# A hybrid decoder step on one core: copies shared by two engines lean to ScalarE, a guard folded into a multiplication, squares cast by ScalarE, and the first steps of the triangular inverses in one instruction each

## The chip, the core and the metric

The kernel runs on one core of a Trainium2 chip. A core has TensorE (PE in the profile, with its weight loads as PEld), VectorE (DVE), ScalarE (ACT), GpSimd (POOL) and SyncE (SP, which only issues DMAs here). Each engine works through its own list of instructions in the order in which the program wrote them, and engines wait for one another by semaphores. The metric is the device time of one execution in microseconds; the profile comes from one further execution.

## The reference, cut to what matters

One decoder layer for a prompt of 1024 tokens and 8 single-token samples: one wide projection of x (1024 features to about 9,360 columns), then two recurrent branches (gated linear attention, "GLA", with 4 heads, and RWKV-7 with 16 heads of 64), a gated merge, an output projection and a layer norm. The part that the change touches is RWKV-7's keys and its recurrence:

```python
kk = hr(kb * rwkv_k_k)
kk = kk / jnp.maximum(jnp.sqrt(jnp.sum(jnp.square(kk), axis=-1, keepdims=True)), L2_EPS)
kb = kb * (1.0 + (a - 1.0) * rwkv_k_a)
...
def step(S, inp):
    rt, wt, kt, vt, kkt, at = inp
    sa = jnp.einsum('bhvk,bhk->bhv', S, -kkt)
    S = S * wt[:, :, None, :] + sa[..., None] * (kkt * at)[:, :, None, :] + vt[..., None] * kt[:, :, None, :]
    y = jnp.einsum('bhvk,bhk->bhv', S, rt)
    return S, y
```

`kk` is each head's key, scaled per channel and normalized over the head's 64 channels, with a guard (`L2_EPS` is 1e-12) against a zero norm.

## The kernel before, in words

All matrix products of the projections are done in three passes with a high and a low part of both operands (`xs` for x, `wpart` for weights; the high part is a rounded copy that ScalarE casts, the low part the difference that VectorE or GpSimd forms). The prompt is worked in two halves of 512 tokens ("contexts" 0 and 1; context 0 carries the 8 samples too, and its rows are 256 and 264 columns wide, while those of context 1 are 512 wide). For each half `make_plan` lists the rows of the projection; between them stand the RWKV pairs (two heads each, 8 pairs per half) and the 4 GLA heads. After the two halves follow the up-projections of both branches (`up_row`) and the output projection with the norm (`out`).

One RWKV pair goes through `pair`: `front` forms decays, normalized keys and the products of the chunked form (chunks of 64 tokens, 8 per half), and solves for 32x32 triangular inverses on VectorE; `back` and `turn` join the blocks and transpose; `chain` walks over the 8 chunks one after the other, and each chunk makes three trips from TensorE to a copying engine and back: `pr` (PSUM tile `pch`) is copied to `rh`, then `pu` is copied to `u` (the tile `wide`; one copy for each head), then `pS` is scaled and added into the next `u` on VectorE. `norm` follows.

In `front`, `head_sums` sums the squared keys over a head with a matrix product by a block matrix of ones: `split` makes a rounded high part and a low part of the squares, each as an own pass of TensorE. The sums come back in PSUM; before, VectorE then takes the maximum with 1e-24, and ScalarE takes logarithm and exponential for the inverse root. The inverse's loop over `j` in `front` makes two VectorE instructions in every step, a product into `Xt` and an addition into `X`. Of its 31 steps the first four have one block row only (`ni == 1`).

The order of the instructions is made by a planner in the file (`Order.run`): streams of operations compete, and the one with the smallest key (start by the planner's own prices, less a priority) is written next on its engine. Operations made through `self.C` can go to ScalarE or VectorE, those through `self.E` to VectorE or GpSimd; `Order.start` takes the way whose end comes first by the planner's prices, after adding `BIAS` to VectorE's end if ScalarE is the first choice:

```python
end = t + cost
if len(op.ways) > 1:
    end += BIAS if eng == "V" and "A" in op.ways[0][0] else ASIDE if eng == "G" and "G" in op.port else 0.0
```

So `BIAS` is the number of planned microseconds by which VectorE must be sooner to get a shared copy. Every choice moves the planned times after it, so the whole order is written anew when one number changes. ScalarE's Sigmoid and Tanh need another table than Exp and Ln; the planner writes the table loads (line 401). Most instructions are written at one line (L217), so groups are told apart by their tiles.

Of the kernel before, what the change touches and what calls it, by code (L numbers as in the profile page):

```python
# [14 lines left out]
AF = mybir.ActivationFunctionType  # L15
ALU = mybir.AluOpType
# [16 lines left out]
C = 64  # L33
# [40 lines left out]

SPARE = 0.4
LANDED = 0.5
BIAS = 0.1
ASIDE = 0.5

PRIO = {"evacuate": 0.7, "pair": 0.4, "turn": 0.5, "chain": 0.5, "norm": 0.1, "x": 0.7, "lora": 0.2, "rank": -0.3,  # L80
# [16 lines left out]
KK_SCALE = 65536.0  # L97
# [325 lines left out]
class Kern(Order):  # L423
# [41 lines left out]
        o, w = CST[name]  # L465
        return self.cons[:, o:o + w]

    def split(self, x, tag="part"):

        hi, lo = (t[:x.shape[0], :x.free_size()] for t in (yield from self.get(tag, 2)))  # L470
        yield self.C.copy(hi, x)
        yield (self.V if x.space == PSUM else self.E).tensor_sub(lo, x, hi.bitcast(F32))
        return hi, lo

# [5 lines left out]
    def blocks32(self, x):  # L480
        return x.rearrange("p (j f) -> p j f", f=32)

    def head_sums(self, x):

        hi, lo = yield from self.split(x)
        ps = yield from self.bank("big", [P, HT])
        yield from self.sums(ps, self.headsr, hi, lo)
        self.free(hi, lo)
        return ps
# [6 lines left out]
    def setup(self):  # L496
        nc, a = self.nc, self.a
        E = mybir.EngineType
        self.es.enter_context(self.tc.manual_schedule(engines={E.PE, E.Activation, E.DVE, E.Pool, E.SP}))
        cp = self.pool("const")  # L500
        wp = self.pool("w", side="left")
        self.dr = self.pool("dr", space=DRAM)
        pp = self.pool("psum", space=PSUM)
        xp = self.pool("x", side="right")
        self.r1 = r1 = self.pool("work", side="left")
        for tag, bufs in BANKS.items():
            self.buffers(tag, bufs, lambda tag=tag, bufs=bufs: pp.tile([P, 512], F32, name=tag, bufs=bufs))
        for tag, (shape, bufs) in SBUF.items():
            dt = F32R if tag in PARTS else F32
            self.buffers(tag, bufs, lambda tag=tag, shape=shape, bufs=bufs, dt=dt:  # L510
                         r1.tile(shape, dt, name=tag, bufs=bufs))
        for tag, (shape, bufs) in WBUF.items():
            dt = F32 if tag == "wraw" else F32R
            self.buffers(tag, bufs, lambda tag=tag, shape=shape, bufs=bufs, dt=dt:
                         wp.tile(shape, dt, name=tag, bufs=bufs))
        self.buffers("xs", XS, lambda: xp.tile([P, HALF], F32R, name="xs", bufs=XS))
        nc.scalar.preload_act_table_set(EXP)
        self.cons = cp.tile([P, CST_W], F32, name="cons")
        self.pv = cp.tile([P, PV_W], F32, name="pv")
        self.ident = self.cst("ident")  # L520
        self.omu = cp.tile([P, NRC], F32, name="omu")
        self.oka = cp.tile([P, 8], F32, name="oka")
        self.nkk = cp.tile([P, 8], F32, name="nkk")
        self.bias = {}
        for n, v in [("glaeps", GLA_EPS), ("gneps", GN_EPS), ("lneps", LN_EPS), ("one", 1.0),
                     ("kkl", 0.5 * math.log(KK_SCALE))]:
            t = cp.tile([P, 1], F32, name="b_" + n)
            nc.vector.memset(t, v)
            self.bias[n] = t
        dbg = getattr(self, "dbg", {})  # L530
        self.o_gla = dbg.get("o_gla", None) or self.dr.tile([D, T], F32, name="o_gla")
        self.o_rwkv = dbg.get("o_rwkv", None) or self.dr.tile([D, T], F32, name="o_rwkv")
        self.sg = [[[self.dr.tile([P, PASS[i][1]], F32, name=f"sg{i}{n}{k}") for k in range(NK)] for n in range(2)]
                   for i in range(2)]
        self.mg = [[self.dr.tile([P, PASS[i][1]], F32, name=f"mg{i}{k}") for k in range(NK)] for i in range(2)]

        self.lev = cp.tile([P, 2 * B32 * MASKED], U8, name="lev")

        self.onesr = cp.tile([P, P], F32R, name="onesr")
        self.headsr = cp.tile([P, P], F32R, name="headsr")  # L540
        self.wa = cp.tile([P, NK * 16], F32, name="wa")
        self.alr = cp.tile([96, HALF], F32R, name="alr")
        self.gw2 = cp.tile([96, GH * GDK], F32R, name="gw2")

        self.GS = [self.dr.tile([P, GDV], F32, name=f"GS{h}") for h in range(GH)]
        self.Sp = [self.dr.tile([P, C], F32, name=f"Sp{n}") for n in range(NPAIR)]

        self.smp = cp.tile([P, 4, NPAIR, NS], F32, name="smp")
        self.RS = self.dr.tile([4, NS, D], F32, name="RS")
        self.WA = self.dr.tile([2, NS, D], F32, name="WA")  # L550
        self.tail = cp.tile([P, NS + 1, NRC], F32, name="tail")
        self.carry = cp.tile([P, NRC], F32, name="carry")
        self.shT = cp.tile([P, NRC, NS], F32, name="shT")
        self.reset = cp.tile([P, HT], U8, name="reset")
        nc.vector.memset(self.reset, 1)
        nc.vector.memset(self.reset[:, ::C], 0)


        for tag, n, bufs in (("XT", 2 * HT, 2), ("X1", HT, 1), ("X2", HT, 1)):
            ts = [cp.tile([P, n], F32, name=f"{tag}{i}") for i in range(bufs)]  # L560
            for t in ts:
                nc.gpsimd.memset(t, 0.0)
            self.fixed(tag, ts)
# [571 lines left out]
    def front(self, c, p, st, d):  # L1135
        a, A, V, E = self.a, self.A, self.V, self.E
# [3 lines left out]
        AZ = az.rearrange("p (c k t) -> p c k t", c=NCH, k=2)  # L1140
# [12 lines left out]
        def bc(ap):  # L1153
            return ap.rearrange("p (c t) -> p c t", t=C)
# [10 lines left out]
        yield from lora(pa, 1)  # L1165
        yield A.activation(td, pa, AF.Sigmoid, bias=self.pvec("a0", p))
        self.free(pa, l2h, l2l)
        ps = yield from self.head_sums(te)
        yield V.tensor_scalar(te, ps, 1e-24, None, ALU.max)
        self.free(ps)  # L1170
        yield V.tensor_tensor_scan(tb, self.reset, ta, 0.0, ALU.mult, ALU.add)
        yield E.memset(Pc[:, :, 0:1], 1.0)
        yield A.activation(te, te, AF.Ln, scale=KK_SCALE)
        yield A.activation(te, te, AF.Exp, scale=-0.5, bias=self.bias["kkl"])
        yield A.activation(Pc[:, :, 1:], bc(tb), AF.Exp, scale=-LAM)
        yield A.activation(tb, tb, AF.Exp, scale=LAM)
        yield V.scalar_tensor_tensor(ta, kb, self.nkk[:, p:p + 1], te, ALU.mult, ALU.mult)
        yield A.activation(te, td, AF.Identity, scale=self.pvec("ka", p), bias=self.oka[:, p:p + 1])
        yield E.tensor_mul(AZ[:, :, 0], bc(ta), Pc[:, :, 0:C])
        yield V.scalar_tensor_tensor(td, td, -1.0, ta, ALU.mult, ALU.mult)  # L1180
        yield E.tensor_mul(kb, kb, te)
        yield E.tensor_mul(AZ[:, :, 1], bc(r), Pc[:, :, 1:])
        pc = yield from self.get("pc")
# [39 lines left out]
        tm = yield from self.get("Xt")  # L1223
        for j in range(31):
            w, ni = 31 - j, j // 4 + 1
            tv = tm[:, :ni * w].rearrange("p (s t) -> p s t", t=w)
            yield V.tensor_mul(tv, X[:, 0:ni, j:j + 1].to_broadcast([P, ni, w]),
                               L[:, j:j + 1, j + 1:].to_broadcast([P, ni, w]))
            yield V.tensor_add(X[:, 0:ni, j + 1:], X[:, 0:ni, j + 1:], tv)
# [70 lines left out]
    def chain(self, c, p, d):  # L1300
# [12 lines left out]
        for x in range(NCH):  # L1313
            u = u_[:, x]
            pr = yield from self.bank("pch", [P, 2, C])
            yield self.P.matmul(pr, GG[:, x, 0], u, start=True, stop=True)
            rh = yield from self.get("rh")
            yield V.tensor_copy(rh, pr)
            self.free(pr)
            s0p = None  # L1320
            if x >= first:
                for h, hs in enumerate(HS):
                    yield A.copy(ss[hs, x], u[hs, h])
                s0p = yield from self.get("s0p")
                yield A.activation(s0p, ss[:, x], AF.Copy, scale=pc[:, x:x + 1])
            pu = yield from self.bank("pch", [P, 2, C])
            yield self.P.matmul(pu, XT[:, x], rh, start=True, stop=True)
            self.free(rh)
            for h, hs in enumerate(HS):
                yield self.C.copy(u[hs, h], pu[hs, h])  # L1330
            self.free(pu)
            pS = yield from self.bank("pch", [P, 2, C])
            yield self.P.matmul(pS, bt_[:, x], u, start=True, stop=True)
            for h, hs in enumerate(HS):
                un = u_[hs, x + 1, h] if x + 1 < NCH else S[hs]
                if s0p is None:
                    yield V.tensor_scalar(un, pS[hs, h], pc[hs, x:x + 1], None, ALU.mult)
                else:
                    yield V.scalar_tensor_tensor(un, pS[hs, h], pc[hs, x:x + 1], s0p[hs], ALU.mult, ALU.add)
            self.free(pS, *([] if s0p is None else [s0p]))  # L1340
# [499 lines left out]
```

## Time and profile before

| what | value |
|---|---|
| time, median of 3 runs | 1490.67 us |
| lowest run | 1490.38 us |
| the profiled execution's own time | 1487.92 us |
| its span, first to last instruction | 1486.1 us |
| granted TensorE clock | 0.996 |
| busy: PE, PEld, DVE, ACT, POOL | 98%, 85%, 80%, 58%, 8% |
| matmuls (PE records) | 11158 |
| table loads of ScalarE | 62 at L401, 1 at L517 |
| DMA traffic | 318.96 MB, mean 215 GB/s |

A row of groups reads: line, engine, operation, output tile<-input tiles, shape, count | busy microseconds in total, mean nanoseconds of one | idle time of the engine just before them and what ended it. A row of waits reads: who waited <- for whom: microseconds in total, times, longest. A row of windows gives the busy time of each engine in a stretch. TensorE's matmuls are pipelined and their ends are modelled, so idle time of PE is a lower bound of its waits.

### The profile page before, as it was taken

The page shows a single profiled execution, that of the slowest core. Times are in us where ns is not written, and L with a number is a line of the kernel's source. Part 1 is how long each engine was busy: PE and PEld are TensorE (multiplying, and loading weights), DVE is VectorE, ACT ScalarE, POOL GpSimd, SP SyncE. Part 2 cuts the span into 40 slices and gives each one's busy share as a digit, 9 for nine tenths or more (in the row PEclk, how much of TensorE's full clock was granted, in tenths as well). Part 3 has the DMA queues.
Part 4 walks back from the last instruction along what each step waited for, and adds up shares of the span by engine and source line. Part 5 has one row for each costly group of instructions (what it writes and reads, how often), then busy time and mean ns, then how long its engine had stood idle before and what let it go on. Part 6 is the DMA issues. An engine that isn't in the chain of part 4 may idle for free. (4 is left out here: it accounts for less than half of the span.)

```text
span 1486.1 us, 31563 instructions
## 1 busy us (share of the span) xinstructions
PE 1449.8 (98%) x11158; PEld 1260.4 (85%) x11158; DVE 1194.8 (80%) x3255; ACT 857.7 (58%) x2196; POOL 113.6 (8%) x208
## 2 busy tenths in 40 slices
PE   9999999999999999999999999999999999999997
PEld 6998999899989998787777777878787898988786
DVE  6697889888998899879878989898877866755665
ACT  5666776676767776665754555474547645544210
POOL 1001010201010102000101020111001000000000
PEclk9999999999999999999999999999999999999999
DMA  8886786678676877566566556656564766888432
GB/s 299 273 285 202 250 296 214 226 253 295 202 258 211 294 229 258 170 224 188 160 198 179 155 190 191 192 154 188 174 189 138 229 210 221 295 293 271 139 107 85
DMA packets 211258, 318.96 MB, mean 215 GB/s; under 512 B 91811, under 2 KB 107180, under 8 KB 211100
## 3 DMA queue, kind: packets, MB, share of 16 engines
q1 hardware_dynamic: 211100, 316.93, 66.8%
q8 instruction: 89, 1.46, 0.4%
q14 instruction: 69, 0.57, 0.1%
HBM read 197.19 MB, written 118.61 MB: 212 GB/s over the span
## 5 line engine op out<-in xcount | busy, mean ns | idle before, releaser
L217 PE MATMUL proj<-xs,wpart 128*128 128x264 f32 (+2 forms) x5640 | 1017.7, 327 | 1.4 <-DVE row L217 0.8
L217 PEld LDWEIGHTS proj<-xs,wpart 128*128 128x128 f32 x5640 | 808.5, 189 | 80.3 <-issue 9.9
L217 ACT CAST wpart<-wraw 128x512 fp32r<-128x512 f32 x210 | 130.2, 623 | 103.5 <-PE proj L217 49.6
L217 DVE TENSOR_TENSOR row<-row 128x512 f32<-128x512 f32 (+7 forms) x321 | 166.3, 524 | 12.4 <-ACT row L217 5.6
L217 DVE TENSOR_TENSOR wpart<-wraw,wpart 128x512 fp32r<-128x512 f32 x207 | 145.2, 702 | 32.3 <-ACT wpart L217 31.4
L217 ACT ACTIVATE row<-row 128x512 f32<-128x512 f32 (+5 forms) x213 | 128.8, 610 | 14.4 <-DMA row<-sg 6.5
L217 POOL TENSOR_TENSOR row<-row 128x512 f32<-128x512 f32 (+5 forms) x64 | 72.7, 1143 | 746.3 <-DVE row L217 396.4
L217 DVE TENSOR_TENSOR Xt<-X,wide 128x60 f32<-128x60 f32 (+24 forms) x496 | 104.8, 211 | 11.7 <-DMA wide<-LD 1.8
L217 DVE TENSOR_TENSOR X<-X,Xt 128x60 f32<-128x60 f32 (+24 forms) x496 | 105.4, 213 | 10.0
L217 ACT ACTIVATE row<-proj,omu 128x256 f32<-128x256 f32 (+1 forms) x99 | 54.0, 546 | 93.5 <-PE proj L217 93.3
L217 PE MATMUL big<-xs,wpart 128*128 128x256 f32 (+2 forms) x576 | 101.7, 332 | 0.0
L217 PEld LDWEIGHTS big<-xs,wpart 128*128 128x128 f32 x576 | 87.7, 194 | 9.7 <-issue 0.2
L217 DVE SCALAR_TENSOR_TENSOR wide<-pch,pc,s0p 64x64 f32<-64x64 f32 x208 | 58.7, 282 | 32.9 <-PE pch L217 28.0
L217 ACT COPY row<-wide 64x64 f32<-64x64 f32 x240 | 57.9, 241 | 40.2 <-DVE wide L217 34.7
L401 ACT ACT_TABLE_LOAD x62 | 79.5, 1283 | 1.1
L217 DVE SCALAR_TENSOR_TENSOR row<-proj,pv,row 128x255 f32<-128x255 f32 (+1 forms) x99 | 56.3, 569 | 22.4 <-ACT tail L217 13.7
L217 PE MATMUL big<-row 128*32 128x32 f32 (+4 forms) x936 | 65.3, 241 | 1.4 <-ACT row L217 1.4
L217 ACT COPY row<-big 128x128 f32<-128x128 f32 (+6 forms) x134 | 38.7, 318 | 42.2 <-PE big L217 36.7
L217 ACT COPY wide<-pch 64x64 f32<-64x64 f32 x159 | 32.8, 206 | 47.0 <-PE pch L217 45.1
L217 ACT ACTIVATE row<-proj 128x128 f32<-128x128 f32 (+4 forms) x136 | 36.9, 324 | 37.4 <-PE proj L217 37.0
L217 PE MATMUL pch<-wide,gg 128*128 128x128 f32 x256 | 51.6, 283 | 5.5 <-DVE wide L217 4.7
L217 PEld LDWEIGHTS pch<-wide,gg 128*128 128x128 f32 x256 | 42.3, 189 | 16.1 <-PE proj L217 4.7
(249 smaller groups left out, 1992.6 us busy)
## 6 DMA issues: line engine op xcount, KB each, us to landing
w<-wpart SPq DMA_DIRECT2D x146, 512.0 KB
wpart<-w SPq DMA_DIRECT2D x146, 512.0 KB
wraw<-w_in SPq DMA_DIRECT2D x146, 256.0 KB
wide<-LD SPq DMA_DIRECT2D x64, 128.0 KB
wraw<-w_up_gla SPq DMA_DIRECT2D x32, 256.0 KB
wraw<-w_up_rwkv SPq DMA_DIRECT2D x32, 256.0 KB
sg<-row SPq DMA_DIRECT2D x16, 260.0 KB
row<-sg SPq DMA_DIRECT2D x16, 260.0 KB
```

The costliest lines, as they stand in the source:

```text
L217: ways.append((eng, lambda call=call: call(out, *args, **kw), price(eng, name, out, args, ins)))
L401: self.nc.scalar.preload_act_table_set(self.table)
```

## The change

Five edits are made.

1. `BIAS` goes from 0.1 to 0.5.
2. The copy to `rh` in `chain`, written for VectorE alone before, becomes a shared copy.
3. For the squared keys, `head_sums` gets a function that writes the rounded high part by ScalarE's Square directly from `kb`; the plain copy (cast) for it goes. The unrounded square stays, for the low part.
4. The maximum with 1e-24 goes, and with it the move from PSUM to SBUF: the logarithm reads PSUM and has a tiny bias. The guard becomes a minimum with 1e12 inside the multiplication that forms `ta`; the factor `rwkv_k_k` moves out of `ta` into the two users: `AZ[:, :, 0]`, a plain product on VectorE or GpSimd before, becomes a fused VectorE instruction with `-kk`, and `td` has `kk` in place of -1.
5. In the inverse's loop the four steps with one block row become one fused instruction each (times a per-partition scalar, plus), with no `Xt`.

```diff
-BIAS = 0.1
+BIAS = 0.5
...
-    def split(self, x, tag="part"):
+    def split(self, x, tag="part", high=None):
         hi, lo = (t[:x.shape[0], :x.free_size()] for t in (yield from self.get(tag, 2)))
-        yield self.C.copy(hi, x)
+        yield high(hi) if high else self.C.copy(hi, x)
...
-    def head_sums(self, x):
-        hi, lo = yield from self.split(x)
+    def head_sums(self, x, high=None):
+        hi, lo = yield from self.split(x, high=high)
...
-                     ("kkl", 0.5 * math.log(KK_SCALE))]:
+                     ("kkl", 0.5 * math.log(KK_SCALE)), ("kkt", KK_SCALE * 1e-34)]:
...
-        ps = yield from self.head_sums(te)
-        yield V.tensor_scalar(te, ps, 1e-24, None, ALU.max)
-        self.free(ps)
+        ps = yield from self.head_sums(te, lambda hi: A.activation(hi, kb, AF.Square, scale=self.pvec("kk", p)))
         yield V.tensor_tensor_scan(tb, self.reset, ta, 0.0, ALU.mult, ALU.add)
         yield E.memset(Pc[:, :, 0:1], 1.0)
-        yield A.activation(te, te, AF.Ln, scale=KK_SCALE)
+        yield A.activation(te, ps, AF.Ln, scale=KK_SCALE, bias=self.bias["kkt"])
+        self.free(ps)
...
-        yield V.scalar_tensor_tensor(ta, kb, self.nkk[:, p:p + 1], te, ALU.mult, ALU.mult)
+        yield V.scalar_tensor_tensor(ta, te, 1e12, kb, ALU.min, ALU.mult)
         yield A.activation(te, td, AF.Identity, scale=self.pvec("ka", p), bias=self.oka[:, p:p + 1])
-        yield E.tensor_mul(AZ[:, :, 0], bc(ta), Pc[:, :, 0:C])
-        yield V.scalar_tensor_tensor(td, td, -1.0, ta, ALU.mult, ALU.mult)
+        yield V.scalar_tensor_tensor(AZ[:, :, 0], bc(ta), self.nkk[:, p:p + 1], Pc[:, :, 0:C], ALU.mult, ALU.mult)
+        yield V.scalar_tensor_tensor(td, td, self.pvec("kk", p), ta, ALU.mult, ALU.mult)
...
             w, ni = 31 - j, j // 4 + 1
+            if ni == 1:
+                yield V.scalar_tensor_tensor(X[:, 0, j + 1:], L[:, j, j + 1:], X[:, 0, j:j + 1], X[:, 0, j + 1:], ALU.mult, ALU.add)
+                continue
...
             rh = yield from self.get("rh")
-            yield V.tensor_copy(rh, pr)
+            yield self.C.copy(rh, pr)
```

What this does to the order is seen at two places. The first is the chain of the last pair of context 1, two of its middle chunks, on the engine that copies `rh`. Before, that is VectorE (`rh<-pch` is the first copy of a chunk, `wide<-pch` the copy of `u`, `wide<-pch,pc,s0p` the update of the next `u`; `wpart<-wraw,wpart` is the low part of a weight block, `row<-big,row` the gating of an up-projection's row):

```order
L217 COPY rh<-pch 128x128
L217 COPY wide<-pch 64x64 x2
L217 TENSOR_TENSOR row<-big,row 128x256
L217 TENSOR_TENSOR row<-row 128x256
L217 SCALAR_TENSOR_TENSOR wide<-pch,pc,s0p 64x64 x2
L217 TENSOR_TENSOR wpart<-wraw,wpart 128x512
L217 COPY rh<-pch 128x128
```

In the changed kernel the same two chunks' copies stand on ScalarE (`row<-wide` and `s0p<-row,pc` were ScalarE's before too; the cast of `wpart` is the high part of a weight block, `row<-row 128x520` a sigmoid of a gate):

```order
L217 COPY rh<-pch 128x128
L217 COPY row<-wide 64x64 x2
L217 ACTIVATE s0p<-row,pc 128x64
L217 COPY wide<-pch 64x64 x2
L217 CAST wpart<-wraw 128x512
L217 ACTIVATE row<-row 128x520
L217 CAST wpart<-wraw 128x512
L217 COPY rh<-pch 128x128
```

The first two of the chunk's three trips moved from VectorE's list to ScalarE's; the update of `u` stays on VectorE. Over the whole program 122 of the 128 copies to `rh` stand on ScalarE, and of the 256 copies `wide<-pch` 253 (159 before).

The second place is VectorE at the start of an inverse in the fifth pair of context 0 (`Xt<-X,wide` is the product, `X<-X,Xt` the addition). Before:

```order
L217 TENSOR_TENSOR Xt<-X,wide 128x31
L217 TENSOR_TENSOR X<-X,Xt 128x31
L217 TENSOR_TENSOR Xt<-X,wide 128x30
L217 TENSOR_TENSOR X<-X,Xt 128x30
L217 TENSOR_TENSOR Xt<-X,wide 128x29
L217 TENSOR_TENSOR X<-X,Xt 128x29
L217 TENSOR_TENSOR Xt<-X,wide 128x28
L217 TENSOR_TENSOR wpart<-wraw,wpart 128x512
L217 SCALAR_TENSOR_TENSOR wide<-pch,pc,s0p 64x64 x2
L217 TENSOR_TENSOR X<-X,Xt 128x28
```

In the changed kernel:

```order
L217 SCALAR_TENSOR_TENSOR X<-wide,X 128x31
L217 SCALAR_TENSOR_TENSOR X<-wide,X 128x30
L217 SCALAR_TENSOR_TENSOR wide<-pch,pc,s0p 64x64 x2
L217 SCALAR_TENSOR_TENSOR X<-wide,X 128x29
L217 SCALAR_TENSOR_TENSOR X<-wide,X 128x28
L217 TENSOR_TENSOR Xt<-X,wide 128x54
L217 TENSOR_TENSOR X<-X,Xt 128x2x27
```

Eight instructions became four; from the fifth step on the pairs of instructions are as before. TensorE's list holds the same 9346 instructions before and after, interleaved differently (2124 rows of like instructions before, 2154 after), and ScalarE's list has 57 table loads in place of 63.

## The prediction

> **What bounds the kernel now.** I read the page's head first, then the windows by stage, then what TensorE waited for, and last the rows of the copies that move.
>
> ```profile
> span 1486.1 us, 31563 instructions
> PE 1449.8 (98%) x11158; PEld 1260.4 (85%) x11158; DVE 1194.8 (80%) x3255; ACT 857.7 (58%) x2196; POOL 113.6 (8%) x208
> ```
>
> TensorE is busy all but 1486.1 - 1449.8 = 36.3 us. The windows show that this is so in every stage, and how loaded the two copying engines are (the columns are busy time in the stretch of PE, PEld, DVE, ACT, POOL, with counts, then granted clock, DMA share and GB/s):
>
> ```profile
> 400.00:500.00 100.00, 96.69 (x962) 91.34 (x960) 90.20 (x245) 72.78 (x197) 12.61 (x26) 1.00 0.73 238
> ...
> 1200.00:1300.00 100.00, 96.04 (x805) 92.24 (x804) 67.77 (x151) 55.19 (x110) 0.00 (x0) 0.97 0.77 248
> 1300.00:1400.00 100.00, 100.00 (x434) 78.82 (x433) 58.57 (x89) 41.70 (x85) 0.37 (x1) 1.00 0.74 249
> ```
>
> In the recurrent stage VectorE is at 90% and ScalarE at 73%; from 1300 us on, the output stage runs with no gap on TensorE at all. So the time can fall only by what TensorE waits. The last matmul and the last instruction of the program bound the tail:
>
> ```profile
> 1477.94 0.51 PE L217 MATMUL big<-wpart,xs 128*128 128x256 f32 x3
> ...
> 1481.65 1.61 POOL L217 TENSOR_TENSOR XT<-XT,az 128x256 f32<-128x256 f32 x2
> ```
>
> From 1477.94 + 0.51 = 1478.45 to 1486.1 are 7.65 us of a tail that the change does not touch. That leaves 36.3 - 7.65 = 28.7 us of waits. Who causes them:
>
> ```profile
> PE pch L217 <- DVE wide L217: 6.0, 9, 1.7
> PE pch L217 <- DVE rh L217: 4.1, 4, 1.8
> PE big L217 <- DVE part L217: 3.0, 5, 0.9
> PE big L217 <- DVE row L217: 2.2, 3, 1.3
> PE big L217 <- POOL XT L562: 1.7, 1, 1.7
> PE big L217 <- DVE X L217: 1.7, 1, 1.7
> PE big L217 <- ACT row L217: 1.4, 2, 1.0
> PE big L217 <- DMA X<-XD: 1.2, 1, 1.2
> PE big L217 <- DVE S L217: 1.1, 3, 0.5
> PE pch L217 <- ACT wide L217: 1.0, 3, 0.5
> PE proj L217 <- DVE row L217: 0.8, 1, 0.8
> PE big L217 <- ACT part L217: 0.7, 1, 0.7
> PE pY L217 <- DVE xs L217: 0.7, 2, 0.5
> ```
>
> VectorE: 6.0 + 4.1 + 3.0 + 2.2 + 1.7 + 1.1 + 0.8 + 0.7 = 19.6 us. ScalarE: 1.4 + 1.0 + 0.7 = 3.1 us. The rest is start, one DMA, and rows of 0.4 us or less. The chain's copies and the squares' parts, which the change touches, are the first three rows. As a matmul's end is modelled, part of a wait is hidden under the matmul before it. The weight load that waits with it shows more:
>
> ```profile
> PEld pch L217 <- DVE rh L217: 6.8, 10, 2.3
> PEld big L217 <- DVE part L217: 5.3, 9, 1.1
> ```
>
> 6.8 against 4.1 and 5.3 against 3.0: (6.8 + 5.3) / (4.1 + 3.0) = 1.7 times. I take that factor for hidden waits, an estimate from these two pairs; the floor is 1.
>
> **The change part by part.** The matmuls stay the same, so no term comes from TensorE's own work; all goes by lateness on the two copying engines. First what VectorE loses (counts from the order, durations from these rows):
>
> ```profile
> L217 DVE COPY rh<-pch 128x128 f32<-128x128 f32 x128 | 37.0, 289 | 17.5 <-PE pch L217 14.7
> L217 DVE COPY wide<-pch 64x64 f32<-64x64 f32 x97 | 21.4, 221 | 13.7 <-PE pch L217 11.3 <-issue 0.3
> L217 DVE COPY wide<-big 64x256 f32<-64x256 f32 x31 | 13.1, 423 | 4.7 <-PE big L217 4.2
> L217 DVE CAST part<-row 128x512 fp32r<-128x512 f32 x31 | 14.8, 477 | 0.4
> L217 DVE TENSOR_SCALAR row<-big 128x512 f32<-128x512 f32 x16 | 11.0, 686 | 4.9 <-PE big L217 4.6
> L217 DVE TENSOR_TENSOR X<-X,Xt 128x31 f32<-128x31 f32 x16 | 4.7, 292 | 0.8
> L217 DVE TENSOR_TENSOR Xt<-X,wide 128x31 f32<-128x31 f32 x16 | 3.0, 185 | 1.9 <-DMA wide<-LD 1.8
> L217 DVE SCALAR_TENSOR_TENSOR wide<-pch,pc,s0p 64x64 f32<-64x64 f32 x208 | 58.7, 282 | 32.9 <-PE pch L217 28.0
> ```
>
> - Copies to `rh`: 122 x 0.289 = 35.3 us. Copies of `u`: 94 x 0.221 = 20.8. Copies `wide<-big` (in `turn`): 27 x 0.423 = 11.4. Some 62 smaller shared copies: at 0.221 to 0.289 each, 14 to 18; I take 14, since most are the smaller tiles.
> - The casts of the squares: 17 x 0.477 = 8.1. The maximum: 16 x 0.686 = 11.0.
> - The inverse's first four steps, 16 pairs, 64 steps: a step of two costs 0.185 + 0.292 = 0.477. The fused one isn't in the trace: not below 0.185, as one of the two still has to run, and the fused instruction with a pointer scalar reads 0.282, though from PSUM. I take 0.28, the costlier end: 64 x 0.20 = 13, or 10, as the longest step has the dearest addition. At 0.185 it would be some 15.
> - Fused in place of plain in `AZ`, and two products that leave GpSimd: under 2 us. `ta` and `td` stay one instruction each; nothing.
> - What the planner shifts besides (16 products from GpSimd and 12 copies from ScalarE come to VectorE, 12 low parts of weights go to GpSimd): about 8 us back, between 0 and 15.
>
> Sum: 35.3 + 20.8 + 11.4 + 14 + 8.1 + 11.0 + 10 - 2 - 8 = some 100 us off VectorE's 1194.8; its idle time rises from 291 to 391 us, by a third. None of these is on TensorE's path by itself: they lie beside the matmuls. Now ScalarE:
>
> ```profile
> L217 ACT COPY row<-big 128x128 f32<-128x128 f32 x64 | 14.5, 268 | 17.8 <-PE big L217 17.6
> L217 ACT COPY wide<-pch 64x64 f32<-64x64 f32 x159 | 32.8, 206 | 47.0 <-PE pch L217 45.1 <-DVE wide L217 0.3
> L217 ACT COPY wide<-big 64x256 f32<-64x256 f32 x33 | 12.1, 367 | 6.0 <-DVE wide L217 5.5
> L217 ACT ACTIVATE row<-row,pv 128x512 f32<-128x512 f32 x16 | 11.6, 725 | 0.0
> L401 ACT ACT_TABLE_LOAD x62 | 79.5, 1283 | 1.1
> L217 ACT ACTIVATE row<-row 128x512 f32<-128x512 f32 x120 | 75.3, 631 | 6.2 <-DVE row L217 2.9 <-DMA row<-sg 2.0
> ```
>
> 122 x 0.268 = 32.7 (the same shape from PSUM), 94 x 0.206 = 19.4, 27 x 0.367 = 9.9, the smaller ones 14, the second Square 16 x 0.725 = 11.6; less 6 table loads, 6 x 1.283 = 7.7, and the 12 copies that left, about 4: 76 us, so 857.7 becomes some 934 (63%). A copy itself is as short as on VectorE (0.268 against 0.289, 0.206 against 0.221); what counts is the queue. A copy that waits for `pch` on ScalarE also holds what stands behind it, the casts of weights and the evacuations of `proj`, for which TensorE waits in turn: by the `wide<-pch` row 47.0 / 159 = 0.30 us of idling each, 216 x 0.30 = 64 us, out of 1486 - 934 = 552 us idle. Covered, unless the engine is late already.
>
> What that is worth on TensorE. The `rh` row goes (4.1). Of the other VectorE waits, 19.6 - 4.1 = 15.5 us, I let a third go, as the idle time grows by a third: 5.2. The bounds are nothing (the waits sit at fixed places) and all. With the hidden part, (4.1 + 5.2) x 1.7 = 16 us. Against it stand new waits for ScalarE: at least none; at most, each of the 216 copies costs what a copy to `rh` cost when VectorE made it, 6.8 / 128 = 0.053 us, 11.5 us. I take half, 6, since ScalarE will be less loaded than VectorE was (63% against 80%), but works in longer pieces (1.283). Shorter ways in `front` (maximum) and inverse gain nothing more: the pairs run ahead of the chain. Net: 16 - 6 = 10 us.
>
> The profiled execution took 1487.92 us, 1.8 more than its span; 10 less gives 1478. The median of the runs is 1490.67, 2.75 above that execution, so I forecast 1481 us.
>
> [...]
>
> **The rivals.**
>
> *A, ScalarE becomes the late one; slower.* TensorE's first two waits of each chunk now hang on one engine that also makes every evacuation, cast and table load. For it: the order puts a cast and a sigmoid, or a table load and three 512-wide activations, between a copy of `u` and the next copy to `rh`. If one of five of the 216 copies is held by one further activation (0.631), that is 43 x 0.631 = 27 us, less the 16 gained: +11, 1502. It decides from 16 / 0.631 = 25 copies on, one in nine. With a table load each (1.283) it would be 43 x 1.283 = 55, less 16: +39, 1530. Against it:
>
> ```profile
> ACT row L217 <- PE proj L217: 153.4, 123, 4.5
> ```
>
> ScalarE mostly stands waiting for TensorE, so it runs ahead. Chance 0.24, of which 0.05 for the heavy form. [...]
>
> *B, nothing moves.* The waits come from each chunk's round trip at the place where the order put it, not from VectorE's load, and ScalarE inherits them. For it: 9 waits make the 6.0 us of the first row, so they are few and particular. Then 1490, give or take 4. Chance 0.16.
>
> *C, nearly all of VectorE's waits go.* 19.6 x 1.7 = 33 us, less 2 of new ones: 1460. For it: with VectorE at 90% in the recurrent stage a little relief may do much. Against it: the update of `u`, in the first row, stays on VectorE. Chance 0.12; of these, 0.02 for the headroom of the weight loads.
>
> That the change doesn't do what it says is excluded by the order.
>
> **How the numbers follow.** The forecast has 0.48; by its own bounds it reaches from 1475 (16 gained, no new waits) to 1486 (11.5 of new ones), with 2 to 3 either way for the factor of hidden waits; A 0.24, B 0.16, C 0.12. The range 1464 to 1502 leaves out half of C and the upper part of A, some 0.16. About 2% is what a measurement of this kernel can tell from no change: below 1461 or above 1520. Faster: half of C, 0.05. Slower: A's heavy form, 0.05. Within: 0.90.
>
> **What would show it.** Right: VectorE near 1095 us and ScalarE near 934, 57 table loads, TensorE's idle time near 30, the row of `pch` waiting for VectorE's `rh` gone, and rows of `pch` waiting for ScalarE's `rh` and `wide` below 4 us together. Wrong: these rows at 10 us and more (A), VectorE's rows as before (B), TensorE's idle time below 18 (C), or a tail other than 7.65 us.

## The result, and the profile after

The changed kernel takes 1480.38 us (median), the kernel before 1490.53 us in the same comparison: ratio 0.9944, 95% interval 0.9926 to 0.9963. The forecast was 1481, within 2%. One of the six runs of before fell in a slow state (1747.76 us) and is left out of the ratio, which stands for some 8 us, where the medians stand 10 apart. The time came out as said; the profile bears out the reason given for it only in part.

The head of the page of the changed kernel:

```profile
span 1482.9 us, 31384 instructions
PE 1445.6 (97%) x11158; PEld 1259.0 (85%) x11158; DVE 1116.0 (75%) x2870; ACT 925.0 (62%) x2502; POOL 104.5 (7%) x202
```

VectorE's busy time lost 79 us (1194.8 to 1116.0; 100 were forecast) and ScalarE's gained 67 (76 were forecast). But TensorE's idle time, the quantity on which the sum was made, is 1482.9 - 1445.6 = 37.3 us, against 36.3 before. The profiled execution of the changed kernel took 1484.72 us, 4.3 above its median, and that of before 1487.92, 2.6 below its own; so the two traces stand only 3.2 us apart, where the medians stand 10 apart. The same kernel profiled again (experiment 5 below) had a span of 1480.1 us and 35.4 us of idle time. In neither is there a fall that would carry 8 to 10 us. What these spans lose stands in TensorE's busy time: 1449.8 before, 1445.6 and 1444.7 after.

Who made TensorE wait, in the changed kernel (rows of 0.6 us and more):

```profile
PE pch L217 <- DVE wide L217: 6.2, 12, 0.9
PE big L217 <- DVE X L217: 4.9, 6, 1.8
PE big L217 <- DMA X<-XD: 3.4, 3, 1.7
PE pch L217 <- ACT rh L217: 2.1, 2, 1.1
PE big L217 <- DVE row L217: 2.1, 4, 1.0
PE big L217 <- POOL XT L562: 1.7, 1, 1.7
PE big L217 <- ACT A L217: 1.3, 2, 1.1
PE big L217 <- ACT row L217: 1.1, 2, 0.9
PE big L217 <- DVE S L217: 1.0, 3, 0.5
PE big L217 <- issue: 0.9, 1, 0.9
PE proj L217 <- DVE row L217: 0.8, 1, 0.8
PE proj L217 <- DVE xs L217: 0.6, 1, 0.6
PE big L217 <- DVE part L217: 0.6, 1, 0.6
```

VectorE: 6.2 + 4.9 + 2.1 + 1.0 + 0.8 + 0.6 + 0.6 = 16.2 us, against 19.6. The wait for VectorE's `rh` (4.1) is gone and that for `part` fell from 3.0 to 0.6, the first as the prediction had it; but waits for the inverse rose (X from 1.7 to 4.9, and its DMA from 1.2 to 3.4), and ScalarE's `rh` makes 2.1. What went in one place came in another.

These rows leave out what is hidden under matmuls, and the prediction had counted on that part. The weight loads show more of it. Summed over all their rows (PEld), their waits for VectorE fell from 26.4 to 20.0 us (15.8 when the same kernel was profiled again), and those for ScalarE rose from 12.7 to 16.3 (16.3). Net that is 2.8 us less (7.0), beside spans that are 3.2 us shorter (6.0). So the waits moved in the direction that was forecast, but by less than the 16 and 6 us of the sum. Whether it was the lower load that moved them, or the new order, only the experiments can tell.

The loads by stage, the same three stretches of 100 us as before:

```profile
400.00:500.00 100.00, 96.72 (x960) 90.98 (x959) 82.92 (x215) 76.53 (x221) 13.55 (x19) 1.00 0.68 214
...
1200.00:1300.00 100.00, 97.25 (x813) 92.97 (x812) 63.06 (x134) 60.03 (x133) 0.00 (x0) 0.98 0.79 250
1300.00:1400.00 100.00, 100.00 (x433) 78.69 (x432) 61.29 (x94) 41.81 (x86) 0.37 (x1) 1.00 0.74 249
```

In the first, VectorE went from 90.20 to 82.92 and TensorE from 96.69 to 96.72: a load 7 us lower went with no more work of TensorE there (960 matmuls against 962). The prices of the single instructions, from the groups by shape:

```profile
L217 DVE SCALAR_TENSOR_TENSOR X<-wide,X 128x31 f32<-128x31 f32 x16 | 4.0, 247 | 5.5 <-DMA wide<-LD 5.3
L217 ACT COPY rh<-pch 128x128 f32<-128x128 f32 x122 | 32.4, 265 | 93.8 <-PE pch L217 93.2
L217 ACT COPY wide<-pch 64x64 f32<-64x64 f32 x253 | 51.9, 205 | 24.3 <-PE pch L217 18.7
L401 ACT ACT_TABLE_LOAD x56 | 71.8, 1283 | 0.9
```

The fused step of the inverse costs 0.247 us (0.28 were taken, between 0.185 and 0.282), the copy to `rh` 0.265 (0.268 taken). ScalarE idles 93.8 us ahead of its `rh` copies, 0.77 each, nearly always for TensorE (93.2).

### The profile page after: what moved, and what is told of

It reads as the page before. It is cut to its first block, busy times and chain, and to the rows that moved or that the text cites. A ratio compares the mean times of both kernels' runs of the same rounds, so it can differ in the third digit from the quotient of the medians.

```text
span 1482.9 us, 31384 instructions
## 1 busy us (share of the span) xinstructions
PE 1445.6 (97%) x11158; PEld 1259.0 (85%) x11158; DVE 1116.0 (75%) x2870; ACT 925.0 (62%) x2502; POOL 104.5 (7%) x202
## 4 chain that ended last, share of the span: by engine, by line
PE 70%; DVE 15%; DMA 5%; SPq 5%; ACT 3%; issue 2%; POOL 0%; POOLq 0%; DVEq 0%; ACTq 0%
PE proj L217 43%; PE big L217 19%; DVE row L217 5%; SPq L217 5%; PE pch L217 5%; PE pY L217 3%; DVE X L217 3%; DVE Xt L217 2%; DVE wpart L217 1%; ACT row L217 1%; DVE wide L217 1%; DMA wraw<-w_in 1%; DMA wide<-LD 1%; DMA X<-XD 1%; DMA XT<-XD 1%
## 5 line engine op out<-in xcount | busy, mean ns | idle before, releaser
L217 PE MATMUL proj<-xs,wpart 128*128 128x264 f32 (+2 forms) x5640 | 1028.0, 328 | 2.3 <-DVE row L217 0.8
L217 DVE TENSOR_TENSOR row<-row 128x512 f32<-128x512 f32 (+7 forms) x332 | 176.4, 538 | 15.4 <-ACT row L217 9.8
L217 DVE TENSOR_TENSOR wpart<-wraw,wpart 128x512 fp32r<-128x512 f32 x195 | 136.1, 701 | 34.6 <-ACT wpart L217 31.4
L217 ACT ACTIVATE row<-row 128x512 f32<-128x512 f32 (+4 forms) x197 | 117.5, 608 | 20.9 <-DVE row L217 12.3
L217 DVE TENSOR_TENSOR X<-X,Xt 128x60 f32<-128x60 f32 (+21 forms) x432 | 97.8, 226 | 9.9
L217 DVE TENSOR_TENSOR Xt<-X,wide 128x60 f32<-128x60 f32 (+21 forms) x432 | 97.0, 225 | 10.5
L217 PE MATMUL big<-xs,wpart 128*128 128x264 f32 (+2 forms) x576 | 100.7, 330 | 0.0
L217 ACT COPY rh<-pch 128x128 f32<-128x128 f32 x122 | 32.4, 265 | 93.8 <-PE pch L217 93.2
L217 POOL TENSOR_TENSOR row<-row 128x512 f32<-128x512 f32 (+5 forms) x53 | 50.8, 965 | 532.7 <-DVE row L217 185.3
L217 ACT COPY wide<-pch 64x64 f32<-64x64 f32 x253 | 51.9, 205 | 24.3 <-PE pch L217 18.7
```

The source lines that it names most:

```text
L217: ways.append((eng, lambda call=call: call(out, *args, **kw), price(eng, name, out, args, ins)))
```

## The experiments

All ratios are to the kernel before on the same chip; each has its 95% interval. The theory at the start was the prediction's: **relief**, TensorE waits less because VectorE has less to do. Its rivals: **fixed places** (rival B), and, new after the result, **arrangement**: every change makes the planner write the whole order anew, and each order has a time of its own.

**1. The copies' move alone** (edits 1 and 2 in the kernel before):

```diff
-BIAS = 0.1
+BIAS = 0.5
...
-            yield V.tensor_copy(rh, pr)
+            yield self.C.copy(rh, pr)
```

> The kernel before with edits 1 and 2 alone (BIAS 0.5, the copy to rh shared): copies move to ScalarE, VectorE's own work stays. Theory of relief (TensorE waits less because VectorE has less to do): these moves are about 70 of the 79 us that VectorE lost, so most of the gain comes with them: 4 to 9 us faster than before. Theory of fixed places: within 2 us of before. Theory of a lucky order (the gain belongs to one arrangement of the instructions): anything from 6 faster to 6 slower, not in proportion to the load.

Measured: 1.0009 (0.9999 to 1.0018), no gain, though VectorE is at 1134.1 us. That fits fixed places as well as arrangement, and not relief. One wait stands out, just after the turn to the second half:

```profile
PE big L217 <- DVE X L217: 6.1, 1, 6.1
```

TensorE stood there for an inverse. And the windows around it show something that the prediction had not priced at all (columns as before; the value after POOL's is the granted clock):

```profile
755.20:768.80 13.60, 9.56 (x41) 7.16 (x39) 12.89 (x32) 8.56 (x16) 2.45 (x2) 1.00 0.50 118
768.80:782.50 13.70, 8.56 (x132) 6.16 (x134) 13.31 (x39) 6.52 (x18) 1.04 (x1) 0.50 0.27 83
782.50:796.10 13.60, 13.60 (x100) 11.73 (x99) 10.50 (x24) 8.10 (x29) 2.41 (x8) 1.00 0.48 112
```

For 13.7 us the granted clock is 0.50.

**2. The removals alone** (the changed kernel with edits 1 and 2 undone: BIAS 0.1, `rh` by VectorE):

> The changed kernel with edits 1 and 2 undone: the maximum, the casts of the squares and half of the inverse's first instructions go, the copies stay on VectorE. Theory of relief: some 25 us less on VectorE, so 2 to 4 us faster than before. Theory of fixed places: within 2 us of before. Lucky order: no relation to the load.

Measured: 1.0026 (1.0015 to 1.0037). Neither half of the change gains by itself, while the whole gains 0.3 to 0.6%. Loads that add up would not do that, and a loss of some 4 us is outside what fixed places allowed.

**3. The order kept, the copies moved.** Here the planner plans the kernel before as it was, and only the instruction that is written at the planned place is another engine's:

```diff
-            op.fn()
+            getattr(op, "emit", op.fn)()
...
-            yield V.tensor_copy(rh, pr)
+            op = V.tensor_copy(rh, pr)
+            op.emit = A.copy(rh, pr).fn
+            yield op
...
-                yield self.C.copy(u[hs, h], pu[hs, h])
+                op = self.C.copy(u[hs, h], pu[hs, h])
+                op.emit = A.copy(u[hs, h], pu[hs, h]).fn
+                yield op
```

> The kernel before with its order kept word for word on TensorE and in the program, but all 128 copies to rh and all 256 copies of u made by ScalarE at the place where the order has them: 37 + 21 us leave VectorE, nothing is planned anew. Relief: 4 to 8 us faster than before. ScalarE becomes late, as the planner did not know of its load: 5 or more slower. Fixed places or lucky order: within 2 us of before.

Measured: 1.0023 (1.0014 to 1.0032), some 3.4 us slower, between the 2 us of fixed places and the 5 of a late ScalarE. TensorE's order is that of the kernel before (of its 11158 matmuls two have changed places). Page and waits:

```profile
PE 1447.6 (97%) x11158; PEld 1258.9 (85%) x11158; DVE 1149.4 (77%) x3030; ACT 898.2 (60%) x2421; POOL 112.6 (8%) x208
```

```profile
PE pch L217 <- ACT wide L217: 5.9, 9, 0.9
PE pch L217 <- DVE wide L217: 5.5, 7, 1.6
PE big L217 <- DVE part L217: 3.3, 6, 1.0
PE big L217 <- POOL XT L562: 1.7, 1, 1.7
PE big L217 <- DVE X L217: 1.7, 1, 1.7
PE pch L217 <- ACT rh L217: 1.7, 2, 1.3
PE big L217 <- DVE row L217: 1.2, 3, 0.7
PE big L217 <- ACT row L217: 1.2, 2, 0.6
```

VectorE does 45 us less (1194.8 to 1149.4), and its rows other than `rh` stand where they stood: `wide` 5.5 (6.0), `part` 3.3 (3.0), X 1.7 (1.7). The 4.1 us for `rh` went over to ScalarE's `rh` and `wide` (1.7 + 5.9, against none and 1.0). The weight loads say the same: their waits for VectorE other than `rh` went from 26.4 - 6.8 = 19.6 to 17.3, those for ScalarE from 12.7 to 26.9. This is the cleanest test of relief here, and relief fails it: the load left, and VectorE's other waits stayed nearly as they were. It has one limit: the planner did not know of ScalarE's new load, and how much of VectorE's waits comes from ScalarE's late copies is not shown.

**4. The changed kernel's order kept, copies given back to VectorE** (all to `rh`, and `u` of one of the two heads):

> The changed kernel with its order kept, but all copies to rh and the copies of u of one of the two heads made by VectorE at the place where the order has them: about 35 + 28 us come back to VectorE. Relief: 4 to 8 us slower than the changed kernel, so 2 to 6 faster than before. Fixed places or lucky order: within 2 us of the changed kernel.

Measured: 1.0187 (1.0173 to 1.0201), 28 us slower than before, which none of the theories had expected. VectorE is at 1180.4 us, still 14 less than in the kernel before:

```profile
PE 1462.5 (96%) x11158; PEld 1258.9 (83%) x11158; DVE 1180.4 (78%) x3119; ACT 870.0 (57%) x2253; POOL 105.9 (7%) x202
```

```profile
PE pch L217 <- DVE wide L217: 16.4, 27, 1.8
PE pch L217 <- DVE rh L217: 4.4, 8, 1.2
PE big L217 <- DVE X L217: 4.0, 4, 1.8
```

The same engine with a lower load than before makes TensorE wait 27 times for `wide` in place of 9 (12 in the changed kernel). So the load alone does not set the waits; what fits is that VectorE has to stand free where the order was planned to find it free.

**5. The changed kernel again**, unchanged, in another comparison.

> The changed kernel once more, unchanged, beside the runs of before on this chip. If its gain is its own and not one chip's: 0.992 to 0.997 of before.

Measured: 0.9968 (0.9955 to 0.9981). The gain is there again, but smaller: with the first, 0.3 to 0.6%.

**6. and 7. A number that has nothing to do with the copies.** SPARE is the slack that the planner adds ahead of a matmul. It was altered in the changed kernel (6) and in the kernel before (7):

```diff
-SPARE = 0.4
+SPARE = 0.42
```

> The changed kernel with one number of the planner altered that has nothing to do with the copies (SPARE 0.42 in place of 0.4, the planned slack ahead of TensorE): the order is written anew, the loads of VectorE and ScalarE stay. If the gain comes from the five edits: 0.992 to 0.997 of before, as the changed kernel. If it belongs to one arrangement: it may land anywhere between 0.990 and 1.006, so a good part of the gain can be gone.

> The kernel before with the same altered number (SPARE 0.42): a new order with the old loads. From the edits: 0.998 to 1.002 of before. From arrangements: it may land anywhere between 0.992 and 1.006; a value below 0.996 would show that a new order alone can gain as much as the change.

Measured: 6: 0.9965 (0.9952 to 0.9978). 7: 0.9932 (0.9912 to 0.9951). The kernel before, with none of the five edits and its loads as they were, gains as much by a new order as the change gained. Its page:

```profile
span 1472.0 us, 31500 instructions
PE 1442.9 (98%) x11158; PEld 1259.0 (86%) x11158; DVE 1190.6 (81%) x3235; ACT 854.6 (58%) x2224; POOL 98.7 (7%) x194
```

TensorE's idle time is 1472.0 - 1442.9 = 29.1 us, with VectorE at 1190.6.

**8. The moves with the shorter inverse** (edits 1, 2 and 5), since in 1 a late inverse had made the longest wait:

> The kernel before with edits 1, 2 and 5 (copies to ScalarE, fused first steps of the inverse). In the trace of edits 1 and 2 alone TensorE stood 6.1 us for an inverse in the pair after the turn to the second half, and its granted clock was 0.5 for 13.7 us there, some 7 us more; that explains why the moves alone gained nothing. If the shorter inverse is what the moves lack: this wait is gone and the kernel lands at 0.992 to 0.997 of before. If arrangements decide: no better than 0.998, with another wait elsewhere.

Measured: 1.0100 (1.0079 to 1.0122), the slowest of all newly planned orders. The idea that the moves lacked the shorter inverse falls: idle time 43.9 us, and three stretches at half clock, together 27.3 us.

**9., 10. and 11. Three more orders**: the kernel before with SPARE 0.38, the changed kernel with SPARE 0.38, and the changed kernel with BIAS 0.4.

> The kernel before with SPARE 0.38: one more new order with the old loads. The kernel before with SPARE 0.42 came out at 0.9932 of before with none of the five edits. Theory of arrangements (each order has a time of its own, which TensorE's idle time and its stretches at half clock account for): anywhere between 0.990 and 1.008, and the span less idle time less half of the stretches at 0.5 within 1439 to 1448 us, as in all runs so far but one. Theory that the edits gain on top of the arrangement: before's arrangements are slower on the mean than those of the changed kernel (0.9944, 0.9968, 0.9965 so far), so this one lies at 0.998 or above.

> The changed kernel with SPARE 0.38: a third order with the new loads. Arrangements alone: between 0.990 and 1.008 of before. A gain by the edits on top: 0.992 to 0.998.

> The changed kernel with BIAS 0.4: nearly the same loads (copies still lean to ScalarE), a fourth order. Arrangements alone: between 0.990 and 1.008 of before. A gain by the edits on top: 0.992 to 0.998.

Measured: 9: 0.9990 (0.9974 to 1.0005). 10: 0.9887 (0.9869 to 0.9904). 11: 1.0054 (1.0036 to 1.0071). With the five edits in and loads alike, the time lies between 0.9887 and 1.0054, over 1.6%. Experiment 9 fits both theories, 10 lies below the ranges of both, and 11 fits arrangement alone. Experiment 10 gives 1471.11 us beside 1487.4 for before on its chip, and is better than both kernels of this case.

**12. Only the inverse's fused steps, the order of before kept** (the planned product is left out, and the fused instruction stands in the addition's place; `op.fn()` is changed as in experiment 3):

```diff
+            if ni == 1:
+                op.emit = lambda: None
...
+            if ni == 1:
+                op.emit = V.scalar_tensor_tensor(X[:, 0, j + 1:], L[:, j, j + 1:], X[:, 0, j:j + 1], X[:, 0, j + 1:], ALU.mult, ALU.add).fn
```

> The kernel before with its order kept word for word, and only edit 5 in it: in the inverse's first four steps the product is left out and the fused instruction stands in the place of the addition. 64 instructions leave VectorE, some 12 us, and each inverse is about 0.9 us shorter. Relief or a shorter inverse: 1 to 3 us faster, since TensorE waits 2.9 us for X and XD in before. Arrangements: within 2 us of before, as with the copies at a kept order.

Measured: 0.9976 (0.9964 to 0.9987), some 3 us faster (medians 1484.3 and 1487.4), at or just above the 1 to 3 us that were expected. TensorE's 11158 matmuls come in the same order as in the kernel before. This is the one edit shown to gain by itself. Why is not shown, for the wait that the shorter chain should have cut stands as it was (X 1.7 before, X<-XD 1.2):

```profile
PE pch L217 <- DVE wide L217: 4.4, 6, 1.4
PE big L217 <- DVE X L217: 1.7, 1, 1.7
PE big L217 <- DMA X<-XD: 1.1, 1, 1.1
```

What is lower is the wait for `wide` (6.0 before), while that for `rh` is 4.7 (4.1 before). So this run can't tell a shorter inverse from a little relief of VectorE (1190.2 us against 1194.8; the fused steps took 0.245 to 0.340 us there). Its trace has a stretch at half clock of 3.4 us in place of 6.8; but over all executions the mean granted clock is 0.9953, and 0.9957 for the kernel before beside it, so the clock is not what gained.

**The account.** From the trace of each run: idle time is the span less the page's busy time of PE; half clock is the sum of the stretches that the trace records with a granted clock of 0.5 ahead of the last matmul. The rest is the span less idle time less half of the stretches, that is TensorE's busy time without what the half clock is estimated to add (half of a stretch, from its granted clock of 0.50).

| kernel | span | VectorE busy | TensorE idle | at half clock | rest |
|---|---|---|---|---|---|
| before | 1486.1 | 1194.8 | 36.3 | 6.8 | 1446.4 |
| 7, before, SPARE 0.42 | 1472.0 | 1190.6 | 29.1 | 3.4 | 1441.2 |
| 9, before, SPARE 0.38 | 1487.9 | 1185.6 | 34.0 | 10.2 | 1448.8 |
| 12, before's order, fused steps | 1480.8 | 1190.2 | 35.1 | 3.4 | 1444.0 |
| 3, before's order, copies moved | 1487.2 | 1149.4 | 39.6 | 0.0 | 1447.6 |
| 1, edits 1 and 2 | 1488.0 | 1134.1 | 38.4 | 20.5 | 1439.3 |
| 2, edits 3 to 5 | 1488.1 | 1172.0 | 39.2 | 10.2 | 1443.8 |
| 8, edits 1, 2 and 5 | 1499.0 | 1128.1 | 43.9 | 27.3 | 1441.4 |
| after | 1482.9 | 1116.0 | 37.3 | 6.8 | 1442.2 |
| 5, after again | 1480.1 | 1115.7 | 35.4 | 3.4 | 1443.0 |
| 6, after, SPARE 0.42 | 1481.6 | 1108.5 | 33.3 | 3.4 | 1446.6 |
| 10, after, SPARE 0.38 | 1470.0 | 1116.7 | 25.8 | 3.4 | 1442.5 |
| 11, after, BIAS 0.4 | 1496.5 | 1110.2 | 43.0 | 23.8 | 1441.6 |
| 4, after's order, copies back | 1515.7 | 1180.4 | 53.2 | 6.8 | 1459.1 |

Without experiment 4 the spans lie 29 us apart and the rest 9.5 us. In experiment 4 the rest is higher, and so are the waits of its weight loads for VectorE and ScalarE (42.5 + 16.6 = 59.1 us, against 26.4 + 12.7 = 39.1 before), which points at waits hidden under matmuls. Over the 14 runs the span goes with idle time plus half of the half-clock stretches (correlation 0.91; 0.95 without experiment 4) and not with VectorE's busy time (0.10; -0.12). Idle time is itself a part of the span, and alone it does as well (0.97; 0.94), so these figures do not prove the price of the clock.

Two limits of the table. A trace is one execution, and executions of one kernel differ: the kernel before took 1481.77 us with a granted clock of 0.998 and 1490.64 with 0.993, on one chip. And the pair of this case differs in the rest alone (1446.4 before, 1442.2 and 1443.0 after, with idle time and half clock nearly alike), so its own gain is not explained by these two columns; the net fall of the weight loads' waits (2.8 and 7.0 us) is the nearest that the traces show.

Is there a gain of the edits on top of the arrangements? Orders of before's loads: 1, 0.9932, 0.9990, mean 0.9974. Orders of the changed kernel: 0.9956 (the mean of its two measurements), 0.9965, 0.9887, 1.0054, mean 0.9966. The means differ by 0.0008, while single orders lie up to 0.017 apart. With so few orders that stays open; a gain of half a per cent by the five edits together is not shown.

## Why the prediction was right, and where its reason was not

**The bound held.** TensorE's own work sets the time in every stage (in the kernel before it is busy for 292.32 to 295.68 us of each 300 up to 1200 us, for 86.27 of the next 90, and for 100.00 from 1300 to 1400 us), so a change that leaves this work as it is could gain only what TensorE loses. In all newly planned orders the time moved by 1.1% down to 1.0% up, with idle time of 25.8 to 43.9 us. That is why the forecast of "within 2%", at 0.90, was safe. That the number came within 1 us of the forecast is luck in good part: the same kernel in another comparison gained 0.3%, some 5 us and not 10, and the kernel before, with nothing but another SPARE, gained 0.7%.

**The ledger held.** VectorE 1116.0 against some 1095, ScalarE 925.0 against 934, 57 table loads, the tail from 1475.20 to 1482.9, 7.7 us. VectorE's missing 21 us are not work that came back. Summed over the rows of the profile its instructions took 1309.3 us before and 1207.0 after, 102 less, as forecast. But the records of neighbouring instructions overlap, and the page's busy time counts an overlap once; so 100 us of durations should not have been taken off the 1194.8 of the page.

**The step that failed** is "Of the other VectorE waits, 19.6 - 4.1 = 15.5 us, I let a third go, as the idle time grows by a third". It turned a load into waits, and its hidden part with the factor 1.7 made 16 us of it. Measured between the two traces, the visible waits for VectorE fell from 19.6 to 16.2, and the weight loads' by 6.4 us (10.6 when profiled again). With the order held, 45 us less on VectorE left its other waits nearly as they were (experiment 3), and an engine with 14 us less than before made TensorE wait for `wide` three times as often (experiment 4). And a new order of the same loads brought as much as the change: in experiment 7 the weight loads' waits for VectorE are 21.0 us with VectorE at 1190.6. So the term was too large, and the rule behind it, waits in proportion to the load, is not borne out.

**The term for ScalarE's new waits** (6 us, at most 11.5) was of the right size where the order is held: ScalarE's rows rose from 3.1 to 5.9 + 1.7 + 1.2 = 8.8 in experiment 3, where `row` stands with 1.2; in the changed kernel to 4.5. The weight loads' waits for ScalarE rose by 3.6 us in the changed kernel, and by 14.2 in experiment 3.

**Rival B** comes nearest in its mechanism ("at the place where the order put it, not from VectorE's load, and ScalarE inherits them"), and experiment 3 agrees with it. In the changed kernel its time, 1490, did not follow; it left out that the places themselves are dealt anew. **Rival A** is seen only in parts: TensorE's visible waits for ScalarE, all rows together, are 3.5 us before, 4.9 in the changed kernel and 12.9 in experiment 8, the most of all. **Rival C** was reached by no run: its time was 1460 with idle time below 18 us, and the fastest run, experiment 10, took 1471.11 with 25.8. The 0.02 that it gave to "the headroom of the weight loads" has no term that a run shows: in the changed kernel, from 1300 to 1400 us, the weight loads are at 78.69 with TensorE at 100.00, so what they leave free there is no wait of TensorE.

**A term that was missing**: the clock. The prediction read the granted clock of 0.97 in the stretch from 1200 to 1300 us and made nothing of it. In the kernel before it is one stretch of 6.8 us at half clock beside the last pair's chain, as the windows of TensorE show (length, busy time, count, granted clock):

```profile
1229.50:1232.90 3.40, 3.40 (x30) 1.00 1.00 337
1232.90:1236.30 3.40, 1.11 (x7) 1.00 0.47 180
1236.30:1243.10 6.80, 6.29 (x30) 0.50 0.67 200
1243.10:1249.90 6.80, 6.80 (x59) 1.00 0.42 136
```

In the timeline of TensorE at the same place (in brackets the idle time ahead) the waits just before are 0.96 and 1.33 us, and ten matmuls of 256 columns take 2.48 us in the stretch and 1.43 us after it:

```profile
1234.18 0.46 PE L217 MATMUL pch<-wide,gg 128*128 128x128 f32 x2 [0.96 <-DVE wide L217]
1235.97 0.54 PE L217 MATMUL pch<-rh,XT 128*128 128x128 f32 x2 [1.33 <-DVE rh L217]
...
1237.47 2.48 PE L217 MATMUL big<-xs,wpart 128*128 128x256 f32 x10
...
1247.49 1.43 PE L217 MATMUL big<-xs,wpart 128*128 128x256 f32 x10
```

So this cluster of waits was paid twice, once as idle time and once by the stretch that follows; that the waits bring the stretch on is the author's reading of the order in time. In the 3.4 us just ahead of this stretch TensorE was still busy 1.11 us, and its longest single wait there was 1.33 us. Not every loss of time has such a stretch behind it: in the same trace TensorE was busy for 1.58 of the 3.4 us from 780.10 us on (one wait of 1.83 us), and the granted clock stayed at 1.00 there and in the 3.4 us after. Half of the stretch is an estimate of the second price, and somewhat high where the ten matmuls stand (2.48 against 1.43 us make 0.42 of it). By the half it goes from 0 (experiment 3) to 13.7 us (experiment 8) over the traces, as much as the whole effect. It does not explain the gain of the change itself, whose trace has 6.8 us at half clock as that of before: two stretches of 3.4 us, against one of 6.8.

## What to carry to other kernels

When an engine at 98% is fed by a written-out order, price an edit on a neighbour by holding the order and changing the one instruction; if the change also rewrites the order, measure two or three neutral rewrites first, for their scatter (here 0.7% to 1.7%) is the noise against which the edit must be read. A lower load on a neighbour is not a gain in itself: with the order held, 45 us moved off VectorE gained nothing, while four fused steps of the inverse gained 0.24%, at a place that the trace does not name. Read the waits of the weight loads beside TensorE's idle time, which leaves out what is hidden under matmuls (in the kernel before, the waits for VectorE's `rh` are 6.8 us on the weight loads and 4.1 on the matmuls). Look for clusters of waits on TensorE as well as for their sum: ahead of each of the 24 stretches at half clock in these traces TensorE had been busy for 2.24 us or less of 3.4, though once in the kernel before 1.58 of 3.4 had no such stretch behind it.

## What the runs showed of the hardware that was not expected

The granted clock went to 0.50 for 3.4 to 13.7 us at a time in 13 of 14 traces ahead of the last matmul, 24 stretches in all. Most of them came without a full stop of TensorE: ahead of 22 of the 24 it was still busy for 0.51 to 2.24 us of the last 3.4 us (3.4 us is the length of the shortest stretch); ahead of the other two (768.8 us in experiment 1, 1229.5 us in experiment 11) for 0.05 us or less. The price shows in the matmuls themselves, 10 of 256 columns in 2.48 us against 1.43.
